# A boost of 400 instead of 100 for the last three searches, and a pace of 3.45 instead of 3.3 for gathers of the last group

## The chip, the cores and the metric

The kernel runs on one core of a Trainium2 chip. The metric is device microseconds (us) of one execution. PE is the matmul engine, DVE the vector engine, ACT the scalar engine, POOL the engine that issues the gathers, SP the engine whose queue issues the plain DMA loads and stores.

## The reference, cut to what matters

One layer of a streaming encoder over 1024 prompt rows and 128 sample rows (9 tiles of 128 rows): a mixer (gating unit and retention), then PEER, a retrieval over 128 x 128 single-neuron experts, and a final norm. What the change touches is PEER:

```python
s1, s2 = q1 . k1, q2 . k2                # 8 heads, 128 keys each
v1, i1 = top_k(s1, 16); v2, i2 = top_k(s2, 16)
vals, flat = top_k(v1[:, None] + v2[None, :], 16)   # of 256 sums
experts = i1[flat // 16] * 128 + i2[flat % 16]      # 16 x 8 = 128 per row
a = gelu(t . eu[experts])
out = sum(softmax(vals) * a * ev[experts])
```

## The kernel before, in words

**Tiles and groups.** The nine tiles go through the trunk (mixer, projection, PEER queries) in three groups, `GROUPS = [[0,1],[2,3,4,5],[6,7,8]]` (L42). PEER is done in two ways. Tiles 0, 1, 2, 6, 7, 8 (`GATHER`) fetch their experts: for each of 128 choices j, one indirect DMA (L865, issued by POOL) brings one 8 KB row of `euv` per partition, 1.05 MB in all. A dot product (L818, DVE), two small ACT steps (L823, L824) and a weighted add (L828, DVE) follow. Tiles 3, 4, 5 (`DENSE`) are multiplied with all experts: a dense phase of 128 steps e (L1028 on), each with 8 matmuls into `S` (L1040), a gelu (L1042, ACT), a product with the weights `pt` (L1044, DVE) and 6 matmuls into `res` (L1053). The weights `pt` are built by `expand` (L871) out of buffers `st` and stored to DRAM (L895) during the last group's trunk.

**Searches.** `topk_units` (L729) finds the experts of one tile. For tiles 0, 1, 2, 6, 7 the 16 best keys of each head are taken inside the trunk (`top_keys`, L716). Tile 8 reads its scores back from DRAM (`load_s`, L741, on SP; two buffers) and takes them in the search. Then come the 64 sums (L757), eight chains of top-16 (L708 to L712 through one buffer `ktmp`), the index arithmetic (L775 to L786), the one-hot products (L794 to L798) and the list `idx` (L802) that the gathers wait for.

**Planner.** Two lanes are traced beside the trunk: gathers and searches. Each lane has a planned time, and the trunk's loop yields planned matmul microseconds (`advance`, L991). `run_side` steps the lane that is due first, until both have reached the trunk's time. A gather adds `PACE[0]` planned us to its lane: 5.0 during the second group, 3.3 from the start of the last group (L1000), 3.55 in the dense phase (L1027).

**Order.** The order on each engine is made when the program is built: among the instructions that are ready there, the one with the lowest trace number goes first. `tc.high_priority(n)` takes n off the numbers of what is traced inside it, and leaves the count outside as it was. The dense phase is traced with 200 off (`DP`, L703). Once all nine tiles have left the trunk, each step of a search is traced with `BOOST[0]` off (L983). That holds for the searches of tiles 6, 7 and 8; those of the dense tiles and the expansions end before it.

**Rings.** A gather takes its buffer from a ring. It has five buffers `gat`; two buffers `st` of the expansion join when the third dense tile is expanded (L953), and one buffer `gax` when the dense phase opens (L1017). From then on gathers name these in turn, and such a gather waits on POOL until its buffer is free.

Of the kernel before, what the change touches and what calls it, by code (L numbers as in the profile page):

```python
# [56 lines left out]
def step_kernel(ctx: ExitStack, tc: tile.TileContext, x, state, wall, wst, bs, rows, vec, cst, smp, cosd, sind, euv,  # L57
# [239 lines left out]
    def trunk(gi):  # L297
        tl = GROUPS[gi]
        nt = len(tl)
        T = nt * P  # L300
        sample = tl[0] == 0

        if gi == 0:
            with tc.tile_pool(name="p0", bufs=1) as pl:
                for _ in front(0, pl):
                    pass
        hT = hTs[gi]
        with tc.tile_pool(name="pm", bufs=1) as pm:
            pb = pm.tile([P, KD, T], F32, name="pb")
            with tc.tile_pool(name="p1", bufs=1) as pl:  # L310
                yield from retention(pl, tl, nt, T, sample, hT, pb)
            with tc.tile_pool(name="p2", bufs=1) as pl:
                mT = yield from gating(pl, tl, nt, T, sample, hT, pb)
        with tc.tile_pool(name="p3", bufs=1) as py:
            tT = pair_tiles(py, T, "y", gi=gi)
            rs = py.tile([P, 4], F32, name="rs")
            with tc.tile_pool(name="p4", bufs=1) as pl:
                unit = yield from project(pl, tl, nt, T, mT, tT, rs)
                flush(True)
            with tc.tile_pool(name="p5", bufs=1) as pl:  # L320
                yield from query(gi, pl, tl, nt, T, tT, rs, unit)
                flush(True)
# [371 lines left out]

    AHEAD = [3]
    PACE = [5.0]
    BOOST = [100]
    AB = 2
    EUB, RWB = 2, 4
    AA = (1, 3)  # L700
# [275 lines left out]
    def run_side(limit):  # L976
        while lanes:
# [3 lines left out]
            try:  # L981
                if len(ready) == NTILE and lane[1] is prep:
                    with tc.high_priority(BOOST[0]):  # L983
                        c = next(lane[1])
# [6 lines left out]
    def advance(c):  # L991
        nonlocal tm
        tm += c
        flush()
        run_side(tm)

    for gi in range(len(GROUPS)):
        if gi == len(GROUPS) - 1:
            ex = ctx.enter_context(tc.tile_pool(name="ex", bufs=1))
            PACE[0] = 3.3  # L1000
        for c in trunk(gi):
            advance(c)
        ready.update(GROUPS[gi])
# [147 lines left out]
```

## Time and profile before

| | |
|---|---|
| median of 3 runs | 3848.13 us (3837.57 to 3850.18) |
| profiled execution | 3852.71 us, its span 3850.9 us |
| busy: PE, DVE, ACT, POOL | 3569.9, 3088.8, 1359.1, 1097.9 us |
| DMA, mean over the span | 335 GB/s |
| DMA, gathers' queue | 822.13 MB |

The page's line of 40 slices is read with the stages in mind. The first group's trunk runs alone at the left. The second and the last group's trunks have gathers beside them, and the dense phase begins at about 60% of the span. From about two thirds on the DMA digits stand at 9 and the rate at 418 to 419 GB/s until the gathers run out, shortly before the end.

### The profile page before, as it was taken

How to read it: one execution, taken by the hardware profiler on the slowest of the kernel's cores; microseconds unless marked ns; L12 is line 12 of the kernel's file. 1: busy time of each engine (PE TensorE's matmuls, PEld its weight loads, DVE VectorE, ACT ScalarE, POOL GpSimd, SP SyncE). 2: the span in 40 equal slices, each digit the busy share in tenths (PEclk: the TensorE clock that was granted, in tenths of full speed). 3: DMA queues.
4: the chain of work that ended last, by engine and by line, in shares of the span. 5: the costliest groups of instructions: out<-in, count | busy, mean ns of one | idle time of the engine just before them, and what ended most of it. 6: DMA issues, size and time to landing. Idle time of an engine off the chain costs nothing.

```text
span 3850.9 us, 45654 instructions
## 1 busy us (share of the span) xinstructions
PE 3569.9 (93%) x15681; PEld 2468.7 (64%) x15681; DVE 3088.8 (80%) x5859; ACT 1359.1 (35%) x3289; POOL 1097.9 (29%) x788
## 2 busy tenths in 40 slices
PE   8999999999989888989999989988999899999998
PEld 6789987877878776767667565544444454444444
DVE  5666699999989789999993679979877877777773
ACT  4455634444343532846545222211112111211111
POOL 0000002433434231132320332334433534443330
PEclk9999999999999999999999989999999999999999
DMA  8675547998989895799994998899999999999993
GB/s 313 238 259 189 195 152 285 363 352 328 359 321 375 340 372 214 246 344 316 365 346 146 369 410 338 337 411 374 418 419 418 419 418 419 419 418 419 418 419 153
DMA packets 300822, 1291.28 MB, mean 335 GB/s; under 512 B 28336, under 2 KB 92592, under 8 KB 200240
## 3 DMA queue, kind: packets, MB, share of 16 engines
q0 software_dynamic: 114944, 822.13, 53.6%
q1 hardware_dynamic: 185648, 466.25, 32.9%
q8 instruction: 124, 2.03, 0.2%
q14 instruction: 106, 0.87, 0.1%
HBM read 1221.16 MB, written 67.11 MB: 335 GB/s over the span
## 4 chain that ended last, share of the span: by engine, by line
DMA 26%; issue 22%; DVE 19%; PE 19%; POOL 11%; ACT 2%; SPq 0%; POOLq 0%; DVEq 0%; ACTq 0%
DMA gat<-in_euv_dram,idx 12%; POOL gat L865 9%; PE gps L210 9%; DMA st<-in_euv_dram,idx 8%; DVE acc L828 5%; PE gps L226 4%; DVE gat L818 3%; PE res L1053 2%; PE S L1040 2%; DMA s<-ssp 1%; DMA gax<-in_euv_dram,idx 1%; POOL st L865 1%; DVE ktmp L710 1%; DVE wlo L240 1%; DVE oh L794 1%
## 5 line engine op out<-in xcount | busy, mean ns | idle before, releaser
L865 POOL DMA_INDIRECT gat<-in_euv_dram,idx x600 | 848.3, 1414 | 1905.0 <-DVE acc L828 1158.3
L828 DVE SCALAR_TENSOR_TENSOR acc<-gat,sdot,acc 128x1024 f32<-128x1024 f32 x600 | 767.0, 1278 | 106.8 <-ACT sdot L824 103.3
L818 DVE CUSTOM_DVE_ANT_0 gat<-gat,tx 128x1024 f32<-128x1024 f32 x600 | 730.1, 1218 | 134.9 <-DMA gat<-in_euv_dram,idx 117.4
L823 ACT ACTIVATE sdot<-sdot 128x1 f32<-128x1 f32 x768 | 154.9, 203 | 1788.3 <-DVE sdot L818 1787.0
L226 PE MATMUL gps<-whi,h 128*128 128x256 f32 x2688 | 519.2, 301 | 6.9 <-ACT h L236 5.7
L226 PEld LDWEIGHTS gps<-whi,h 128*128 128x128 f32 x2688 | 437.7, 193 | 28.2 <-issue 10.1
L226 PE MATMUL gps<-wlo,h 128*128 128x256 f32 x1536 | 419.6, 312 | 8.8 <-issue 5.5
L210 PE MATMUL gps<-h,whi 128*128 128x256 f32 (+2 forms) x1520 | 407.4, 366 | 4.6 <-ACT th L591 3.2
L210 PE MATMUL gps<-y,whi 128*128 128x256 f32 (+2 forms) x1168 | 310.7, 362 | 9.4 <-DVE pb L382 4.8
L226 PEld LDWEIGHTS gps<-wlo,h 128*128 128x128 f32 x1536 | 295.9, 194 | 26.9 <-issue 13.0
L210 PEld LDWEIGHTS gps<-h,whi 128*128 128x128 f32 x1520 | 270.7, 193 | 62.3 <-ACT th L591 3.8
L210 PE MATMUL gps<-h,wlo 128*128 128x256 f32 (+2 forms) x864 | 292.8, 378 | 6.6 <-DVE wlo L240 6.4
L1040 PE MATMUL S<-h,wlo 128*128 128x384 f32 x672 | 252.3, 509 | 41.6 <-ACT g L1042 41.6
L1040 PE MATMUL S<-h,wraw 128*128 128x384 f32 x688 | 258.6, 510 | 29.0 <-ACT g L1042 28.4
L865 POOL DMA_INDIRECT st<-in_euv_dram,idx x118 | 164.7, 1396 | 370.5 <-DVE acc L828 229.4
L1040 PE MATMUL S<-h,whi 128*128 128x384 f32 x688 | 248.7, 493 | 21.7 <-ACT g L1042 21.6
L1053 PE MATMUL res<-wraw,g 128*128 128x512 f32 x516 | 243.1, 594 | 1.7 <-DVE g L1044 1.7
L1053 PE MATMUL res<-wlo,g 128*128 128x512 f32 x516 | 243.7, 592 | 0.5 <-DVE g L1044 0.5
L1040 PEld LDWEIGHTS S<-h,wlo 128*128 128x128 f32 x672 | 132.7, 200 | 170.0 <-issue 65.0
L1053 PE MATMUL res<-whi,g 128*128 128x512 f32 x504 | 240.1, 595 | 0.9 <-DVE g L1044 0.9
L210 PEld LDWEIGHTS gps<-y,whi 128*128 128x128 f32 x1168 | 206.4, 192 | 51.9 <-issue 7.4
L1040 PEld LDWEIGHTS S<-h,wraw 128*128 128x128 f32 x688 | 135.8, 199 | 158.5 <-issue 67.6
(230 smaller groups left out, 5686.7 us busy)
## 6 DMA issues: line engine op xcount, KB each, us to landing
wraw<-in_wall_dram SPq DMA_DIRECT2D x214, 512.0 KB
gat<-in_wall_dram SPq DMA_DIRECT2D x84, 512.0 KB
pdr<-st SPq DMA_DIRECT2D x24, 1024.0 KB
pt<-pdr SPq DMA_DIRECT2D x16, 1536.0 KB
wlo<-in_wall_dram SPq DMA_DIRECT2D x43, 512.0 KB
whi<-in_wall_dram SPq DMA_DIRECT2D x43, 512.0 KB
wraw<-in_eud_dram SPq DMA_DIRECT2D x43, 512.0 KB
whi<-in_eud_dram SPq DMA_DIRECT2D x43, 512.0 KB
```

Source lines behind the costliest of these rows:

```text
L210: mm(ps[:, c, :T], x, y, start=kh == 0 and k == 0 and j == 0, stop=kh == nk - 1 and k == 3 and j == len(pr) - 1)
L226: mm(ps[:, i], y, x, start=kh == 0 and k == 0 and j == 0 and i % 2 == 0, stop=kh == 1 and k == 3 and j == len(pr) - 1 and last)
L240: nc.vector.tensor_tensor(parts[1], src, parts[0].bitcast(F32), op=OP.subtract)
L710: nc.vector.match_replace(tmp, v[:, :8], src, -3.0e38)
L794: tt(oh, ij[:, c, hs, None].to_broadcast([P, n, TOPK]), iota[:, None, :].to_broadcast([P, n, TOPK]), op=OP.is_equal)
L818: nc.vector.tensor_tensor_reduce(out=b[:, :D], in0=b[:, :D], in1=d["x"], op0=OP.mult, op1=OP.add, scale=1.0, scalar=0.0, accum_out=d["s"][ ...
L823: nc.scalar.activation(d["s"][:, j:j + 1], d["s"][:, j:j + 1], AF.Gelu_apprx_tanh)
L828: nc.vector.scalar_tensor_tensor(d["acc"], b[:, D:], d["s"][:, j:j + 1], d["acc"], op0=OP.mult, op1=OP.add)
L865: nc.gpsimd.indirect_dma_start(out=b, out_offset=None, in_=euv, in_offset=bass.IndirectOffsetOnAxis(ap=d["idx"][:, j:j + 1], axis=0))
L1040: mm(ps, w[:, k * P:(k + 1) * P], tT[:, k], start=k == 0, stop=k == KD - 1)
L1053: mm(res[n, j], g[:, n * P:(n + 1) * P], w[:, 512 * j:512 * j + 512], start=e == LEAD, stop=e == NKEYS + LEAD - 1)
```

## The change

The number taken off the trace numbers of the searches behind the trunk becomes 400 instead of 100. The planned cost of a gather during the last group's trunk becomes 3.45 us instead of 3.3. No instruction is added or removed.

```diff
     AHEAD = [3]
     PACE = [5.0]
-    BOOST = [100]
+    BOOST = [400]
     AB = 2
@@
         if gi == len(GROUPS) - 1:
             ex = ctx.enter_context(tc.tile_pool(name="ex", bufs=1))
-            PACE[0] = 3.3
+            PACE[0] = 3.45
         for c in trunk(gi):
             advance(c)
```

## Rows read from the trace of the kernel before

**Rows 1.** Windows: length, busy PE, PEld, DVE, ACT, POOL, clock, DMA share, GB/s
```profile
1760.00:2020.00 260.00, 239.25 (x1012) 171.86 (x1011) 237.52 (x497) 140.62 (x357) 77.22 (x57) 0.95 0.95 347
2020.00:2117.00 97.00, 94.45 (x455) 71.79 (x454) 37.98 (x99) 56.69 (x133) 0.00 (x0) 0.98 0.49 147
2117.00:2381.00 264.00, 230.01 (x849) 153.46 (x847) 206.33 (x449) 73.83 (x230) 99.83 (x67) 0.94 0.97 389
2381.00:2520.00 139.00, 134.57 (x368) 69.75 (x368) 126.52 (x344) 26.82 (x72) 40.76 (x30) 1.00 0.82 319
2520.00:2660.00 140.00, 113.83 (x282) 56.84 (x283) 112.66 (x295) 21.46 (x81) 59.39 (x36) 0.90 0.98 386
2660.00:3765.00 1105.00, 1040.29 (x2742) 528.31 (x2741) 859.29 (x1126) 207.10 (x755) 438.40 (x321) 0.98 1.02 418
```
**Rows 2.** The same windows, dense products L1044 on DVE alone, one per step e
```profile
2520.00:2660.00 140.00, 5.79 (x11) 0.90 0.98 386
2660.00:3765.00 1105.00, 53.68 (x99) 0.98 1.02 418
```
**Rows 3.** The same windows, gathers L865 on POOL alone
```profile
1760.00:2020.00 260.00, 77.22 (x57) 0.95 0.95 347
2117.00:2381.00 264.00, 99.83 (x67) 0.94 0.97 389
2660.00:3765.00 1105.00, 438.40 (x321) 0.98 1.02 418
```
**Rows 4.** Page, costliest groups: busy, mean ns of one, idle before, releaser
```profile
L828 DVE SCALAR_TENSOR_TENSOR acc<-gat,sdot,acc 128x1024 f32<-128x1024 f32 x600 | 767.0, 1278 | 106.8 <-ACT sdot L824 103.3
L818 DVE CUSTOM_DVE_ANT_0 gat<-gat,tx 128x1024 f32<-128x1024 f32 x600 | 730.1, 1218 | 134.9 <-DMA gat<-in_euv_dram,idx 117.4
```
**Rows 5.** Waits of POOL, 1760 to 2020 and 2020 to 2130: total, times, longest
```profile
POOL gat L865 <- DVE acc L828: 119.7, 38, 12.9
...
POOL st L865 <- DMA pdr<-st: 97.3, 1, 97.3
```
**Rows 6.** Waits of PE, 1760 to 2020 (two), 2117 to 2381 (one)
```profile
PE sps L892 <- ACT ab L917: 9.9, 4, 4.5
PE sps L892 <- DVE ab L902: 5.0, 1, 5.0
...
PE sps L619 <- DVE x L634: 9.6, 1, 9.6
```
**Rows 7.** Timeline of POOL around the trunk's end: start, duration, [idle before, releaser]
```profile
2393.08 0.94 POOL L865 DMA_INDIRECT gax<-in_euv_dram,idx  x1 [26.47 <-DVE iu L712]
...
2434.47 1.15 POOL L865 DMA_INDIRECT gat<-in_euv_dram,idx  x1 [24.26 <-DVE idx L802]
```
**Rows 8.** Timeline of DVE: first and last step of tile 6's search, one add between
```profile
2381.42 0.54 DVE L757 TENSOR_TENSOR cand<-v 128x192 f32<-128x192 f32 x2
...
2404.33 1.27 DVE L828 SCALAR_TENSOR_TENSOR acc<-gax,sdot,acc 128x1024 f32<-128x1024 f32 x1
...
2433.98 0.22 DVE L802 CAST idx<-m 128x128 int32<-128x128 f32 x1
```
**Rows 9.** Waits of the SP queue, 2520 to 2740 us
```profile
SPq L741 <- DVE ktmp L710: 50.0, 4, 12.8
SPq L741 <- DVE v L708: 27.6, 1, 27.6
```
**Rows 10.** Tile 8's score loads, L741: ns min/median/max, first and last start
```profile
L741 SPq DMA_DIRECT2D s<-ssp x32: 319/327/3840, 1446.9 to 2616.6; - x32
```
**Rows 11.** Chain that ended last: two pieces behind the last gather, and its end
```profile
3780.51 0.65 PE S L1040 x2
3781.16 0.86 PE res L1053 x2
...
3822.83 13.75 PE res L1053 x32
```
**Rows 12.** Timeline of POOL: the last gather
```profile
3760.10 1.68 POOL L865 DMA_INDIRECT gat<-in_euv_dram,idx  x1 [2.47 <-DVE acc L828]
```

## The prediction

> **What bounds the kernel now.** I read the busy times by stage first, then who each queue waits for at the places the change touches, then the chain at the end.
>
> The last group's trunk ends near 2381 us. Up to 2020 us PE is busy 239 of 260 us and DVE 238 of 260 [rows 1]: PE sets the pace, and DVE is nearly full beside it. Gathers are what DVE does in its spare time there: POOL's largest wait is for the weighted add that frees a buffer, 119.7 us in that stretch [rows 5]. Then POOL stands 97.3 us for one event, the last store of the expansion, which frees the first `st` buffer [rows 5]. In the 97 us from 2020 no gather is issued, DMA falls to 147 GB/s and PE runs best, 94.5 of 97 us [rows 1]. From 2117 to 2381 the 67 gathers [rows 3] make DMA full, 0.97 at 389 GB/s, and PE falls to 230 of 264 us [rows 1].
>
> The dense phase has three parts. From 2660 to 3765 DMA is full, 418 GB/s [rows 1], and 99 steps e [rows 2] and 321 gathers [rows 3] pass: 1105/99 = 11.16 us per step, 3.24 gathers per step, 3.44 us per gather. After the last gather (3760 us [rows 12]) only PE is left. Two `S` pieces take 0.65 us and two `res` pieces 0.86 [rows 11], and a step has 16 and 12 of them: 16 x 0.323 + 12 x 0.43 = 10.33 us, PE's own pace. So beside gathers a step costs 0.83 us more than PE needs. The middle part, 2520 to 2660, is worst: 11 steps in 140 us [rows 2], 12.7 each, PE busy 114 of 140 and DMA at 386 GB/s [rows 1]. There SP stands 50.0 + 27.6 us before loads of tile 8's scores, whose buffers DVE has not freed [rows 9], and weight loads queue behind. Against 11.16 us that part loses 140 - 11 x 11.16 = 17 us.
>
> **The change part by part: the pace.** The planner's sums can be done by hand from the yields. In planned us the last group's trunk runs from 1223 to 1952, the third expansion ends at 1743, and tile 1's gathers (109 are left) end at 1587. At 3.3, 304 gathers are handed out by 1743 and 367 by 1952. At 3.45, tile 1's end at 1603, and the counts are 297 and 357. So 7 fewer come before `st` joins the ring, 3 fewer between that and `gax`, 10 fewer in all before the dense phase. The 10 return in the dense phase.
>
> How far does the order follow the plan? Not closely: 57 gathers ran from 1760 to 2020 us [rows 3], 4.6 us each, where POOL waited for DVE [rows 5]. A later trace number takes nothing from an instruction that already fills gaps. What binds is the ring: the first `st` gather stops POOL until 2117 whatever its number, the first `gax` gather until 2393 (a wait of 26.47 us, which other DVE work released [rows 7]). The pause now comes 7 gathers earlier, and POOL reaches `gax` 10 gathers earlier.
>
> First term, ahead of the pause: a gather costs DVE 1.22 + 1.28 = 2.50 us [rows 4], so 7 take 17.5 us out of a stretch in which DVE is 91% busy. PE's waits for the expansion's operands there are 9.9 + 5.0 us [rows 6], the most that can come back: 0 to -15. The store that ends the pause is behind PE's expansion matmuls, and PE is near full, so I take -3.
>
> Second term, 2117 to 2381: 3 gathers fewer of 1.05 MB, at 418 GB/s 2.51 us each, 7.5 us of DMA time, and POOL stops at `gax` sooner. PE's wait on x, which comes by DMA, is 9.6 us [rows 6], so 0 to -10. I take -2.
>
> Third term, 10 gathers more in the dense phase. At the price of DMA alone that is 25 us, the upper bound. But a step whose gathers are gone drops to 10.33 us: 10/3.24 = 3.1 steps pass from the short to the long form, 3.1 x 0.83 = 2.6 us. PE works 77 us past the last gather [rows 11, 12], room for 77/3.44 = 22 more. Part of the ten is free: POOL stands 24.26 us for tile 6's list [rows 7], and from 2381 to 2520 DMA moved 319 GB/s [rows 1], (418 - 319) x 139 us = 13.8 MB, 13 gathers short of full. DVE had 139 - 126.5 = 12.5 us left there [rows 1], 5 gathers at 2.50. The other 5 cost half of 2.6: +1.3, bounds 0 and +25.
>
> The Trainium skill (DMA: Bandwidth & Descriptors, section Anatomy of one DMA — SWDGE (gpsimd) path) gives a transfer from POOL's queue about 2.0 us plus its bytes at 436 GB/s. By this estimate a gather is 4.4 us, ten are +44 us if none overlap, and the sum would be slower. The trace disagrees with that reading: 321 gathers took 3.44 us each, with the weights beside them.
>
> **The boost.** Boosted steps leave the outer count alone, and a gather is 5 traced instructions, so 100 is 20 gathers in the dense phase and 400 is 80 (less in the trunk, whose instructions count too).
>
> Tile 6's search: it starts at 2381.4, as soon as its last keys are there, and ends at 2434.0 [rows 8]. Adds of tile 2's gathers lie between its steps, though they are traced after it: each step needs the one before, and DVE takes what is ready meanwhile. Its number is already the lowest of these. If the whole wait of 24.26 us [rows 7] went, 7 gathers would move forward, 7 x 0.83/3.24 = -1.8 us; if dense products wait behind it, +3 (six of 0.53 us, 53.68/99 [rows 2]). They are used one to two steps later, so I take 0.
>
> Tile 7's search now comes ahead of the dense products too (400 against 200). Its list isn't needed until gather 512, long after. 0.
>
> Tile 8's search is traced at gather 520. It now counts as if at 440, before at 500. Its last score load goes out at 2616.6 us [rows 10]; with tile 6's first gather, number 384, at 2434.47 [rows 7] and 3.44 us each, that is beside gather 437. So its keys run beside gathers that still come first. So its loads on SP, their waits and the 17 us stay: 0, bounds -17 (stall gone) and +25 (below).
>
> The sum: -3 - 2 + 1.3 + 0 = -3.7, say -4. The profiled execution took 3852.7 us, 0.12% above the median of 3848.1: 3848.7 on its own scale, 3844 against the median.
>
> **Rivals.** (1) The trunk takes all the relief: -15 - 10 = -25, 3823 us. For it, DVE is full and POOL waits on it [rows 5]; against it, PE's named waits are small. (2) The stall of tile 8 goes, because its keys now beat gathers: -17, 3831. For it, 440 is only just behind 437; against, those still have the lower numbers. (3) Slower: the displaced gathers' dots and adds land in tile 8's key stretch. Its six later heads each finish one gather (2.50 us) later, SP's loads wait that much longer, and dense weights queue behind them: 6 x 2.5 = +15, 3863. It decides once SP's waits at L741 pass 77.6 + 11.5, some 89 us; the weights loaded ahead cover less. For it, SP's order is fixed and DVE has 12.5 us left for 25 us of work; against, POOL's ring also delays those gathers. (4) It doesn't do what it says: gathers fill gaps and searches are first anyway, and nothing moves: 3848. (5) By the skill's rule as read above, all in series, +44, 3892; the rows refuse it, 0.02.
>
> **How the numbers follow.** A measurement can tell about 0.3% here (11.5 us, so 3836.6 to 3859.7). The forecast has 0.44, rival 4 0.10; both are within: same 0.54. Rival 1 has 0.14 and rival 2 0.14: faster 0.28. Rival 3 has 0.16, rival 5 0.02: slower 0.18. The predicted time is the forecast's, 3844. The range runs from a little below rival 1, 3818, to a little above rival 3, 3867, leaving out sums of rivals and rival 5.
>
> **What would show it.** Right: POOL's pause begins some 15 to 30 us earlier and ends near 2117; some 10 fewer gathers stand ahead of the first `gax`; tile 6's list comes near 2430, and POOL waits less than 24 us for it; the last gather comes 10 to 35 us later, the last matmul moves little; SP's waits at L741 stay near 78 us. Wrong: the first dense product comes more than 10 us earlier (rival 1), or steps between 2520 and 2660 come at 11.2 us (rival 2) or at 14 (rival 3).

## The result, and the profile after

The changed kernel takes 3824.3 us (median of 9 runs, 3817.26 to 3834.95) against 3846.87 us for the kernel before (9 runs, 3832.99 to 3853.36). The ratio is 0.995, with a 95% interval of 0.9936 to 0.9963: 0.5% faster, some 20 us.

The page of the changed kernel, span and busy times:

```profile
span 3821.5 us, 45663 instructions
PE 3553.1 (93%) x15681; PEld 2459.3 (64%) x15681; DVE 3090.3 (81%) x5859; ACT 1359.1 (36%) x3288; POOL 1092.3 (29%) x788
```

PE does the same 15681 matmul records in 17 us less busy time, in a span that is 29 us shorter; DVE's work is the same. So PE waits less in this execution, and is faster while it works.

POOL around the two places where the ring stops it. Its longest wait from 1760 to 2130 us (total, times, longest):

```profile
POOL st L865 <- DMA pdr<-st: 118.7, 1, 118.7
```

And its timeline (start, duration, idle before and its releaser):

```profile
1973.67 1.14 POOL L865 DMA_INDIRECT gat<-in_euv_dram,idx  x1 [0.66 <-DVE acc L828]
2093.52 0.94 POOL L865 DMA_INDIRECT st<-in_euv_dram,idx  x1 [118.71 <-DMA pdr<-st]
...
2364.43 0.94 POOL L865 DMA_INDIRECT gax<-in_euv_dram,idx  x1 [34.09 <-DVE iu L712]
...
2421.26 1.87 POOL L865 DMA_INDIRECT gat<-in_euv_dram,idx  x1 [0.79 <-DVE pos L712]
```

The pause is 118.7 us, 97.3 before [rows 5]. It begins after 307 gathers (314 before), as the plan's sums said. The first `gax` gather waits 34.09 us (26.47 before [rows 7]). The last row is gather 384, the first of tile 6: it has no wait for its list any more (24.26 us before [rows 7]), because 13 gathers of tile 2 are still to come at the first `S` matmul (3 before).

For the times of stages I take the same instructions as bounds in every profile: a matmul in the last group's trunk (at 1750.1 us in the first profile of before), the last store of the expansion, the start of the first `S` and of the last `res` matmul. The windows below have the columns of [rows 1]. First the kernel before: up to the expansion's last store, the rest of the trunk, and the dense phase.

```profile
1750.10:2130.30 380.20, 356.90 (x1564) 259.36 (x1563) 289.12 (x640) 210.57 (x515) 80.25 (x60) 0.96 0.81 289
2130.30:2381.40 251.10, 216.71 (x797) 144.93 (x795) 203.01 (x445) 68.69 (x220) 97.95 (x65) 0.94 0.99 399
...
2381.40:3837.70 1456.30, 1361.39 (x3584) 691.68 (x3584) 1121.07 (x1792) 261.60 (x927) 538.56 (x387) 0.97 0.96 391
```

The changed kernel, the same three:

```profile
1727.60:2105.30 377.70, 353.19 (x1558) 255.91 (x1557) 272.90 (x584) 209.17 (x507) 75.97 (x56) 0.96 0.77 277
2105.30:2351.80 246.50, 216.44 (x803) 144.79 (x801) 195.79 (x430) 67.41 (x213) 92.64 (x62) 0.94 0.97 394
...
2351.80:3808.30 1456.50, 1357.60 (x3584) 689.02 (x3584) 1146.05 (x1829) 265.40 (x946) 545.78 (x397) 0.98 0.97 398
```

The trunk's part shrinks from 631.3 to 624.2 us. The dense phase is as long as it was, with 397 gathers in it instead of 387. The first bound itself lies 22.5 us earlier. Nearly all of that lead can't come from the change: up to 1692 us of the changed kernel every engine's instructions and SP's loads come in the same order as before, and a matmul close behind begins at 1696.1 us against 1718.4 before. It is the luck of one execution, as the repeats below show.

### The profile page after: what moved, and what is told of

The parts are those of the page before. It is cut to its first block, busy times and chain, and to the rows that moved or that the text cites. A ratio compares the mean times of both kernels' runs of the same rounds, so it can differ in the third digit from the quotient of the medians.

```text
span 3821.5 us, 45663 instructions
## 1 busy us (share of the span) xinstructions
PE 3553.1 (93%) x15681; PEld 2459.3 (64%) x15681; DVE 3090.3 (81%) x5859; ACT 1359.1 (36%) x3288; POOL 1092.3 (29%) x788
## 5 line engine op out<-in xcount | busy, mean ns | idle before, releaser
L865 POOL DMA_INDIRECT gat<-in_euv_dram,idx x597 | 850.9, 1425 | 1863.6 <-DVE acc L828 1153.2
L1040 PE MATMUL S<-h,whi 128*128 128x384 f32 x688 | 256.9, 508 | 35.1 <-ACT g L1042 35.0
L865 POOL DMA_INDIRECT st<-in_euv_dram,idx x120 | 158.6, 1321 | 390.4 <-DVE acc L828 229.7
L1040 PE MATMUL S<-h,wlo 128*128 128x384 f32 x672 | 241.5, 493 | 21.5 <-ACT g L1042 16.0
L1040 PEld LDWEIGHTS S<-h,whi 128*128 128x128 f32 x688 | 134.8, 198 | 164.8 <-issue 61.8
```

The source lines that it names most:

```text
L865: nc.gpsimd.indirect_dma_start(out=b, out_offset=None, in_=euv, in_offset=bass.IndirectOffsetOnAxis(ap=d["idx"][:, j:j + 1], axis=0))
L1040: mm(ps, w[:, k * P:(k + 1) * P], tT[:, k], start=k == 0, stop=k == KD - 1)
```

## The experiments

All ratios are against the kernel before, with a 95% interval.

**The two edits apart, and both kernels once more.** The boost alone:

```diff
-    BOOST = [100]
+    BOOST = [400]
```

> The boost of 400 alone, pace 3.3 as before. Theory P (the pace brings the gain, by a shorter trunk of the last group): no change, ratio to the kernel before 0.997 to 1.003. Rival B (the boost brings it, by shorter waits of SP for tile 8's scores): ratio about 0.994, with SP's waits at L741 clearly below 78 us. The gathers' order on POOL is that of before, so the 24 us wait for tile 6's list should stay.

Measured: 0.9998 (0.9987 to 1.0008). The order on POOL is that of before, and tile 6's first gather still waits for its list (POOL's timeline):

```profile
2420.94 1.15 POOL L865 DMA_INDIRECT gat<-in_euv_dram,idx  x1 [21.92 <-DVE idx L802]
```

The pace alone:

```diff
-            PACE[0] = 3.3
+            PACE[0] = 3.45
```

> The pace of 3.45 alone, boost 100 as before. Theory P: ratio about 0.995, the first dense matmul 5 to 10 us earlier than in a run of the kernel before that began alike, and no 24 us wait for tile 6's list. Rival B: ratio 0.998 to 1.003.

Measured: 0.9951 (0.9939 to 0.9963). The pace's gain is that of both edits together, and the boost's can't be told from nothing. SP's waits for tile 8's score loads, from 2340 to 2770 us (total, times, longest), here:

```profile
SPq L741 <- DVE v L711: 62.9, 4, 19.8
...
SPq L741 <- DVE v L708: 33.4, 2, 24.8
```

And in the changed kernel:

```profile
SPq L741 <- DVE v L711: 24.4, 2, 15.4
SPq L741 <- DVE v L708: 24.3, 3, 12.7
SPq L741 <- DVE ktmp L710: 13.9, 1, 13.9
```

That is 96.3 us against 62.6 us, with the same time.

The kernel before once more:

> The kernel before once more, for a second profile. In the first two profiles the changed kernel led by 20 us before the last group's trunk, where both have the same order. If that lead is the luck of one execution, this profile differs from the first by some 10 to 20 us at that point and the ratio is 1.000. If it belongs to the program, this profile stands there where the first did, within 5 us.

Measured: 1.0004 (0.9994 to 1.0014). The changed kernel once more:

> The changed kernel once more, for a second profile: ratio 0.995. If the 20 us lead ahead of the last group's trunk is luck, it differs here; if it belongs to the program, it is there again, within 5 us.

Measured: 0.9961 (0.9948 to 0.9974). The first bound lies at 1750.1, 1743.0 and 1736.0 us in the three profiles with the pace of before (before twice, boost alone), and at 1727.6, 1741.5 and 1745.8 in the three with 3.45. The two sets overlap, so the lead was luck. From there to the first `S` matmul the first three take 631.3, 633.0 and 632.7 us, the others 624.2, 618.0 and 620.8. The sums of the trunk's two windows (length, then busy times), before again:

```profile
sum 633.00, PE 572.44 PEld 403.44 DVE 491.90 ACT 279.10 POOL 179.55; mean PE 286.22 PEld 201.72 DVE 245.95 ACT 139.55 POOL 89.77
```

The changed kernel again:

```profile
sum 620.80, PE 570.50 PEld 401.87 DVE 469.41 ACT 276.57 POOL 167.36; mean PE 285.25 PEld 200.93 DVE 234.70 ACT 138.29 POOL 83.68
```

Of the 12.2 us, 10.3 are time in which PE stood (633.0 - 572.4 = 60.6 against 50.3).

**Where the trunk gains.** In the stretch that runs from 1962 to 2117 us in the first profile of before, by the same matmuls. Before:

```profile
1962.00:2117.00 155.00, 147.48 (x691) 112.44 (x690) 86.93 (x177) 89.88 (x226) 19.70 (x14) 0.97 0.68 231
```

The changed kernel, second profile:

```profile
1966.50:2110.30 143.80, 143.80 (x699) 110.03 (x698) 73.58 (x163) 88.54 (x217) 11.50 (x9) 1.00 0.62 205
```

With 14 gathers beside it this piece of program takes PE 155 us, with 9 it takes 143.8 us, and PE then doesn't stand for a moment. Two things went: 7.5 us of waiting, nearly all for the expansion's operands `ab` from DVE and ACT (5.0 + 2.4 us), and 3.7 us of busy time, as the granted clock goes from 0.97 to 1.00. In the kernel before, the clock is at half (0.50, the 1.2 GHz level) around the end of the wait of 5.0 us, which ends at 2008.2:

```profile
2006.00:2012.00 6.00, 3.79 (x13) 3.46 (x14) 4.83 (x10) 0.50 (x2) 0.82 (x1) 0.50 1.00 331
```

This piece isn't the whole account. Ahead of it, from the first bound, the trunk loses 7 us (211.9, 213.7 and 211.6 us with the pace of before, 220.7, 217.3 and 220.7 with 3.45). Before, and the changed kernel again:

```profile
1750.10:1962.00 211.90, 196.12 (x822) 138.39 (x821) 198.47 (x458) 115.19 (x280) 58.67 (x44) 0.96 0.93 336
...
1745.80:1966.50 220.70, 196.09 (x814) 137.42 (x814) 196.01 (x417) 115.13 (x281) 61.74 (x47) 0.95 0.89 329
```

PE is as busy there and stands 9 us longer; why is open. (Eight matmuls of the expansion move from there into the piece above, which is why it has 699 records and 691 before.) Behind the piece, up to the first `S` matmul, the trunk gains 6 us (264.2, 262.7 and 262.7 against 257.9, 256.8 and 256.1). Five of them come just ahead of the first `S` matmul, where PE waits for `qh` before and not in the three profiles with 3.45 (before, 2336 to 2420 us):

```profile
PE sps L655 <- ACT qh L672: 3.8, 1, 3.8
```

So the trunk's 11 us are 7 lost, 12 gained in the pause and 6 gained behind it.

**Is it the ring or the trace numbers?** Pace and boost as before, but `st` and `gax` enter the ring at its front:

```diff
-                    rings_.extend([(ex, "st", 2)] * 2)
+                    rings_[:0] = [(ex, "st", 2)] * 2
...
-    rings_.append((gx, "gax", 1))
+    rings_.insert(0, (gx, "gax", 1))
```

> The kernel before, pace 3.3 and boost 100 untouched, but the buffers st and gax enter the ring of gathers at its front instead of its end, so that POOL stops for st after 309 gathers (314 before) and for gax after 374 (381 before). Theory R (the pace works only through the place of these stops: what pays is that fewer gathers run beside the trunk): 7 of the 10 gathers, so about two thirds of the gain, ratio 0.9965 (0.995 to 0.998). Rival N (the pace works through the trace numbers of all gathers in the trunk): 1.000.

Measured: 0.9968 (0.9956 to 0.9981). No gather's planned time was touched, the stops come after 309 and 374 gathers, and the trunk's part fell to 618.9 us. So the two stops give the gain. Ahead of the pause this kernel loses nothing (213.5 us in the stretch that took 211.6 to 213.7 before and 217.3 to 220.7 with 3.45): those 7 us come with the planned times, which the change moves too.

**The pause taken away.** `st` joins only when the dense phase opens:

```diff
-                    rings_.extend([(ex, "st", 2)] * 2)
-                    AHEAD[0] += 2
+                    pass
...
-    rings_.append((gx, "gax", 1))
-    AHEAD[0] += 1
+    rings_.extend([(ex, "st", 2)] * 2 + [(gx, "gax", 1)])
+    AHEAD[0] += 3
```

> The kernel before, but st joins the ring only when the dense phase opens, so that POOL does not stop for it in the trunk: there is no pause near 2020 us, and gathers run on to 384, tile 2's last. If every gather beside the trunk costs PE the same, 3 more of them make no difference: 0.999 to 1.003. If the pause itself is what lets PE run, because gathers crowd up behind it and cost less there, slower, about 1.004. If the crowd behind the pause is what hurts, faster, about 0.996.

Measured: 1.0013 (0.9998 to 1.0027). The gathers run on to 2272 us and then stand (POOL's timeline):

```profile
2394.11 0.94 POOL L865 DMA_INDIRECT gax<-in_euv_dram,idx  x1 [119.89 <-DVE iu L712]
```

The piece of program shown above, its window here (it runs 1.8 us past the matmul that ends it):

```profile
1960.70:2140.00 179.30, 154.96 (x697) 116.75 (x696) 146.51 (x253) 98.51 (x275) 59.01 (x41) 0.92 0.94 348
```

PE's waits in that window (total, times, longest):

```profile
PE sps L892 <- DVE ab L902: 18.4, 4, 7.2
PE sps L892 <- DVE ab L912: 4.1, 1, 4.1
PE sps L892 <- ACT ab L917: 1.6, 2, 1.2
```

With 41 gathers the piece takes 177.5 us to that matmul, 33.7 more than with 9: 1.1 us for each gather, as a mean. It isn't a fixed price: the step from 9 to 14 gathers cost 2.2 us each, that from 14 to 41 0.8. PE waits 24.1 us for `ab`, and the granted clock is 0.92. The pause isn't a loss for PE but its best time. It comes back at the other place, where the gathers now stand 119.9 us. With the same 381 gathers ahead of the first `S` matmul the trunk's part is 639.6 us, 7 longer than before, so it counts where they run and not only how many. The time as a whole can't be told from before.

**What does a gather cost in the dense phase?** Tile 8 leaves out 20 of its 128 choices, so its result lacks them:

```diff
-        for j in range(HK):
+        for j in range(20 if t == 8 else 0, HK):
```

> The kernel before, but tile 8 leaves out its first 20 of 128 choices, so that the dense phase has 20 gathers fewer and everything ahead of them is as before; tile 8's result lacks these. It measures what a gather in the dense phase costs. By the price of DMA time, 2.51 us each: 50 us, ratio 0.987. By the price of the step (0.83 us more per 3.24 gathers while they last): 5 us, ratio 0.9987 (0.997 to 1.000), with the last gather some 69 us earlier and the last matmul nearly where it was.

Measured: 1.0001 (0.9992 to 1.001). The dense phase's window:

```profile
2372.90:3831.60 1458.70, 1363.88 (x3584) 692.90 (x3584) 1072.00 (x1732) 252.41 (x887) 514.08 (x367) 0.97 0.92 376
```

Its last gather on POOL's timeline:

```profile
3686.07 0.94 POOL L865 DMA_INDIRECT gat<-in_euv_dram,idx  x1 [2.84 <-DVE acc L828]
```

POOL is through 74 us earlier than before, and the phase takes 1458.7 us with 367 gathers, where before took 1456.3 and 1458.7 with 387. By the interval these 20 gathers are worth at most 0.08%, 3 us, or 0.15 us each. The windows from 3690 to 3760 us, here without a gather on POOL:

```profile
3690.00:3760.00 70.00, 64.70 (x172) 33.13 (x171) 21.55 (x29) 7.06 (x22) 0.00 (x0) 0.98 0.43 154
```

And in the kernel before, with 20:

```profile
3690.00:3760.00 70.00, 64.70 (x172) 33.20 (x171) 53.98 (x68) 12.45 (x47) 25.14 (x20) 0.95 1.02 418
```

PE is busy 64.70 of 70 us in both. What it waits for there is the same one wait in both profiles, ahead of step 116 (it ends at 3696.2 us here and at 3702.0 before; the last gathers' adds still run on DVE here):

```profile
PE S L1040 <- ACT g L1042: 5.3, 1, 5.3
```

Behind it, beside 17 of its last 18 gathers, PE in the kernel before doesn't wait at all:

```profile
3703.00:3760.00 57.00, 57.00 (x153) 29.58 (x153) 45.01 (x58) 10.34 (x39) 22.32 (x17) 0.98 1.02 418
```

So the gathers left out had held nothing up. This prices gathers at the end of the phase, which is where the change adds its ten. It doesn't price those from 2660 to 3690 us, where PE waits 58.5 us for the gelu `g`.

**How far does it go?** The changed kernel with 3.9:

```diff
-            PACE[0] = 3.45
+            PACE[0] = 3.9
```

> The changed kernel with a pace of 3.9: 333 gathers planned ahead of the dense phase, 34 fewer than before. Theory R: each gather taken from the trunk gives back 1.1 to 1.2 us and costs almost nothing in the dense phase as long as the last gather comes before the end: ratio about 0.991. The room behind the last gather (91 us before, 68 with the change) shrinks to about 15 us. Rival (the ten gathers only closed the 24 us wait for tile 6's list, and more buys nothing): 0.995, or over 1.000 if the last gather passes the end.

Measured: 1.0086 (1.0064 to 1.0107). The trunk's part is 613.1 us and the last matmul begins at 3815.5, but the gathers end behind it. The dense phase's window:

```profile
2348.90:3815.50 1466.60, 1365.75 (x3584) 691.69 (x3584) 1174.77 (x1866) 270.68 (x972) 598.76 (x418) 0.97 1.00 408
```

The last two gathers on POOL's timeline:

```profile
3838.01 1.74 POOL L865 DMA_INDIRECT st<-in_euv_dram,idx  x1 [18.88 <-DVE rfin L250]
3841.61 1.68 POOL L865 DMA_INDIRECT st<-in_euv_dram,idx  x1 [1.86 <-DVE acc L828]
```

The span ends 52.3 us after the last matmul begins, 13.3 before. The expectation had 15 us of room left: it took 2.3 us of room per gather from the change's ten, and the 34 took 3.0 each (77.6 us ahead of the last matmul before, 26 behind it here), and 18.9 us of that are one wait of POOL for a step of the final norm. With 3.6:

```diff
-            PACE[0] = 3.45
+            PACE[0] = 3.6
```

> The changed kernel with a pace of 3.6: 349 gathers planned ahead of the dense phase, 18 fewer than before and 8 fewer than with the change. The room behind the last gather shrinks by 2.3 us for each: from 55 us to some 35, and the tail of tile 8 still fits. Theory R: the trunk of the last group 2 to 5 us shorter than with the change, the dense phase the same: ratio 0.994. If the trunk gave all it has at 10 gathers: 0.9955. If the last gather already sets the end: over 0.997.

Measured: 0.9969 (0.9956 to 0.9981), no better than with 3.45. The trunk's part is 617.8 us, no shorter than with 3.45 in the pace's and the changed kernel's later profiles (618.0 and 620.8), and the last gather goes out at 3789.17, so late that the span ends 18.3 us after the last matmul begins. The trunk had given nearly all with the first ten, and the tail already costs 5 us.

**The stall of SP's queue.** Six buffers for tile 8's scores, in the kernel before:

```diff
-                sc[h] = peer.tile([P, 2 * P], F32, name="s12", bufs=2)
+                sc[h] = (peer.tile([P, 2 * P], F32, name="s12", bufs=2) if t != 8 or h in (4, 5) else
+                         gx.tile([P, 2 * P], F32, name="s8", bufs=4))
...
-            load_s(0)
-            load_s(1)
+            ahead = 6 if t == 8 else 2
+            for h in range(ahead):
+                load_s(h)
...
-                load_s(h + 2)
+                load_s(h + ahead)
```

> The kernel before with six buffers instead of two for the scores of tile 8, loaded six heads ahead, so that SP's queue no longer stands behind DVE there. If those waits (78 us in all) hold back the dense weights as the prediction costed it, the 17 us that the stretch from 2520 to 2660 us loses come back: ratio 0.9955, and its steps come at about 11.2 us. If the stretch is slow because DMA and DVE are full there anyway, 1.000, with the waits gone.

Measured: 0.9987 (0.9974 to 1.0001). SP's longest waits from 2360 to 2740 us for those loads (one line lower in this kernel):

```profile
SPq L742 <- DVE v L708: 30.0, 1, 30.0
SPq L742 <- DVE wg L811: 12.1, 1, 12.1
```

The dense phase's window:

```profile
2372.70:3820.60 1447.90, 1357.45 (x3583) 690.07 (x3584) 1122.45 (x1795) 261.73 (x927) 543.43 (x387) 0.98 0.96 393
```

One wait of 30.0 us is left of 77.6, and one of 12.1 us is new. Counted from the first `S` matmul, step 28 begins at 304 us (319 and 321 before), which is the 15 to 17 us that the prediction had priced. At the last step the lead is 8 to 11 us, and the timed runs show about 5, with an interval that reaches no change. So the waits that went cost at their place what was read for the whole stall, and part of it is taken back later. The time lies between the two expectations and can't be told from the second, no change.

On the changed kernel:

> The changed kernel with six buffers for the scores of tile 8, as in e6. That alone gave 0.9987, the change 0.995 to 0.996; if they act on different stretches they add up: 0.9940. If DMA is full in that stretch and takes the gain back: 0.9955.

Measured: 0.9943 (0.993 to 0.9956), median 3821.71 us; its dense phase takes 1444.9 us in the profile. The interval holds both expectations. With 3.6:

> Pace 3.6, boost 400 and six buffers for the scores of tile 8 together: 0.9930 if all three add up, 0.995 if the end is already set by the last gathers.

Measured: 0.995 (0.9936 to 0.9963), as if the end is already set by the last gathers. The first of the two is the fastest version by its median, but its interval overlaps the change's own, so the timing doesn't tell them apart.

## Why the prediction was right or wrong

The measured time lies in the range, 20 us below the forecast of 3844 us; the likeliest case was no measurable change, and the change is 0.5%. The time is that of rival 1 (the trunk takes all the relief, 3823 us, chance 0.14), and its sign came (the first dense product 12 us earlier from the first bound, by the means of three profiles). But rival 1 had 25 us from the trunk and the trunk gave 11, so that the number fits it so closely is luck.

- **The counts held.** 7 gathers fewer ahead of the pause (307 against 314), 10 fewer ahead of the first `S` matmul (371 against 381), the wait for tile 6's list gone. So rival 4 (nothing moves) is out. That the pace binds through the ring held too: moving the ring's entries alone gave 0.9968.
- **First and second term, the trunk: mis-sized.** I took -3 and -2 with bounds -15 and -10. Measured between the same matmuls, the trunk's part gives 7 to 15 us, 11 by the means of three profiles each (632.3 and 621.0). Split at the matmul that stands at 2117 us before, the first term is -5 and the second -6. The bounds were right and the values weren't. The step that failed first was to take PE's waits for the expansion's operands as the most that can come back. In the pause these waits go whole (7.5 us in the piece shown), and PE's busy time falls as well (3.7 us, clock 0.97 to 1.00), which no row of waits shows. By the means of three profiles each that gives 12 us, and the loss ahead of the pause takes 7 of them. I had read that PE ran best in the pause and didn't price it: at 0.8 to 2.2 us a gather, seven are 6 to 15 us. In the second term PE's wait on `x` was the wrong row: its releaser is an add on DVE (L634), and 7.8 to 9.1 us of its 9.6 are still there with 3.45. What went is the wait for `qh`, which the rows didn't show.
- **Third term, ten gathers in the dense phase: small, as said, but for another reason.** +1.3 was taken; three profiles with 397 gathers give 1456.5, 1455.3 and 1454.2 us against 1456.3, 1458.7 and 1461.5. Its price of 0.26 us for each gather took a step beside gathers to be slower throughout. Beside the last gathers of the kernel before PE doesn't wait at all (busy 57.00 of 57.00 us), and 20 gathers fewer gave at most 0.15 each. The DMA's full 2.51 us is refused, and with it rival 5's price in series. The room of 22 gathers counted to the last matmul only and was too large: with 18 moved, 29 us are left between the last gather and the last matmul, and the end is already 5 us later.
- **The boost at 0: right,** 0.9998. Tile 6's search still takes 52 us from its first sums to its list. DVE is busy 45.1 of these 52.0 us with the boost alone, so there was little waiting to take away.
- **Rivals 2 and 3:** SP's waits at L741 were 62.6 us in the changed kernel for the stall that was 77.6, so they neither went nor grew past 89. With the pace alone they were 96 us, and the time was the same. So the point from which rival 3 was to decide was wrong.

Of some 20 us the matched stages show about 11 in the trunk and 3 in the dense phase. The profiles' lead at the first bound, 4.7 us by the means of three each, isn't the change's: 4.5 of it stand at the last matmul up to which the order is the same. The timed gain has an interval of 14 to 25 us, and the repeat of the changed kernel gave 0.9961, 15 us. So no more than the 15 us that the stages show is shown to be the change's.

## What to carry to other kernels

Background work costs what it delays where it runs, not its bytes. Beside a matmul stage that waits for small operands from DVE and ACT, a gather cost PE 0.8 to 2.2 us; at the end of a stage where PE didn't wait beside gathers, twenty of them cost less than 3 us together. So here it paid to hand such work to the second stage, up to the point where its end sets the end of the whole: ten moved gathers gave 0.5%, 18 no more than that, and 34 lost 0.9%. And when a planner's pace is changed, look for what turns it into order; here it was the place in a ring where the next buffer isn't free.

## What the runs showed of the hardware

- Where PE had short waits, its granted clock was lower: the same piece of program had 1.00 and 143.8 us busy without a wait, 0.97 and 147.5 us with 7.5 us of waits, 0.92 and 153.2 us with 24.1 us. Around the end of a wait of 5.0 us the clock stood at 0.50.
- With DMA at 418 GB/s, twenty gathers of 1.05 MB could be left out at the end of the phase without shortening it. A full DMA share didn't mean that the end hung on DMA.
- Executions with the same order on every engine differ by up to 22 us at one matmul (1696.1 to 1718.4 us over six profiles), so stages of single profiles have to be compared between the same instructions.
